# Low parts of split operands by accumulating DMAs on GpSimd, and a new list of priorities for the order, in a decoder trunk kernel

## The chip, the cores and the metric

The kernel runs on one core of one Trainium2 chip. The metric is device time in microseconds (us) from the launch of the program to its end, as a median over runs; lower is better. Beside it stands one execution under the hardware profiler, which gives the start and end of nearly every instruction on the five engines: TensorE (PE; its weight loads are shown as PEld), VectorE (DVE), ScalarE (ACT), GpSimd (POOL) and SyncE (SP, which here issues DMAs only).

## The reference

One layer of a decoder trunk on a sequence of 1024 tokens with 1024 channels, all in float32. The input is normalised, projected to 6 x 256 columns, given to four mixers of 256 channels each, projected back, added to a scaled copy of its own input and normalised; then comes a gated feed-forward net with a short causal convolution, and again a sum and a norm.

```
h  = x @ w_in + b_in              # 1024 x 1536: S5 | conformer value, gate | RG-LRU gate, input | query
A  = s5_mixer(...)                # complex diagonal state space, scan over time, GLU
B  = conformer_conv(v, g, ...)    # GLU, causal depthwise conv of 31 taps, group norm, swish, pointwise
C  = rglru_branch(xg, xr, ...)    # conv of 4 taps, block-diagonal gates, scan, gelu gate
M  = memory_cross_attention(q, mem, w_kv)   # 4 heads, 256 memory tokens
x  = layer_norm(alpha * x + concat(A, B, C, M) @ w_out, ...)
u  = causal_dwconv(x @ w_up);  ffn = (val * gelu(gt)) @ w_down        # d_ff = 2816, conv of 3 taps
x  = layer_norm(alpha * x + ffn, ...)
```

## The kernel before

**Stages.** Eight tiles of 128 tokens are loaded (`x0` to `x7`), normalised, turned by 64 PE transposes of 128x128 into a channel-major copy in PSUM, and split. Every large product takes float32 operands as a high part (rounded to the PE's fp32r type, `xh`, `wh`, `mxh`) and a low part (what the rounding left, `xl`, `wl`, `mxl`), and adds three passes: high x high, high x low, low x high (`mm3`). The in-projection runs over 12 column blocks of 128 (`in_mm`, n = 0 to 11; names `in_0`, `in_1` are the two halves of a block in PSUM), 48 matmuls of 128x512 each. Between its blocks stand the mixers: S5 (`s5_setup`, `s5_weights`, `s5_states`: PE products `vr`, `vi` of the turned input `ut`, scans `s5r`, `s5i` on VectorE, then `yp` products), the RG-LRU (`xr`, its four-tap convolution `xc`, gates `gt`, scan `gs`, output `lg`), the conformer (31 taps, of which 60 multiply-adds `acc` of 1.27 us run on VectorE and the rest on PE as `cc`; group norm with the products `cvar` and `cb` around a GpSimd power `crs`), and attention (`kps` and `vps` are keys and values of the memory, `sc`, `pt`, `ot` scores, transposes and outputs). Then the out-projection (`out_mm`, tiles `op`, i = 0 to 7 blocks of tokens, 8 k-steps), its residual `r1` and norm, and the feed-forward net as two Strassen-like products of seven block products each (`ux`, `ua`, `ub` up, `dna` to `dnc` down), whose operand sums run on VectorE.

**The low part.** In `split_w` a weight block of 128x1024 that a DMA has brought to `ws` is rounded to `wh` (by ScalarE or VectorE) and VectorE subtracts: `wl = ws - wh`. The same subtraction makes the low parts of the mixers' outputs: `put` (S5 glu and RG-LRU), `conf_out` and `attn_out`. In `residual` the input tile is reloaded, VectorE multiplies it by `g0r` and adds the row `bor` (names `r<-r,g0r` and `r<-r,bor`).

**What sets the order.** All work is first recorded in a `Plan`, as operations with a cost, their dependences and their buffers. `run` then places them one after the other, on each engine the operation that can start soonest and, within 0.1 us, the one with the largest critical path plus a number from the table `BOOST`, which has an entry for each part of the program (`in_mm`, `attn0`, `residual3`, ...). Operations recorded with `either` (all plain copies) go to ScalarE or to VectorE as the plan finds it. Each engine then issues its list strictly in that order, so an instruction that waits holds up all that stands behind it on its engine; SP's and GpSimd's lists of DMAs too. All instructions are emitted from one line, so every row of the profile says L405, and rows are told apart by their tiles.

Of the kernel before, what the change touches and what calls it, by code (L numbers as in the profile page):

```python
# [12 lines left out]
F32 = mybir.dt.float32  # L13
F32R = mybir.dt.float32r
I32 = mybir.dt.int32
AF = mybir.ActivationFunctionType
ALU = mybir.AluOpType
# [18 lines left out]
for _n, _w in (("b_in", 12), ("g0", 8), ("b0", 8), ("b_glu", 2), ("cv_w", 62), ("cv_b", 2),  # L36
# [18 lines left out]
TABLE = {AF.Exp: "exp", AF.Sigmoid: "sigmoid", AF.Gelu_apprx_tanh: "gelu", AF.Silu: "silu", AF.Sqrt: "sqrt", AF.Sin: "sin"}  # L55
TICK = 10240 / 3

BOOST = {"attn0": 109000, "attn1": -40000, "attn2": 27000, "attn3": -5000, "attn4": -35000, "attn5": 111000, "attn6":
# [18 lines left out]
         "up_post": 60000, "up_prep": 3500, "up_sums": 6500, "worse": 76}  # L77
LATENCY = {"tensor": 0, "vector": 120, "scalar": 150}


# [8 lines left out]
class Plan:  # L89
# [82 lines left out]
    def add(self, eng, method, a, kw, chain=None):  # L172
        aps = [v for v in list(a) + list(kw.values()) if hasattr(v, "ap") and hasattr(v, "offset")]
        out = kw.get("out", a[0] if a else None)
        outs = [out] + ([kw["accum_out"]] if "accum_out" in kw else [])
        ins = [v for v in aps if not any(v is o for o in outs)]
        o = self.open
        if o is None or o.eng not in (None, eng):
            o = Op()
            o.eng, o.calls, o.cost, o.lat, o.succ, o.npred, o.tiles, o.table, o.bytes, o.dge, o.part, o.work = eng, [], 0, 0, {}, 0, [], None, 0, 0, self.name, []  # L180
            o.alts = {}
            o.idx = len(self.ops)
            self.ops.append(o)
            if self.open is not None:
                self.open = o
        elif o.eng is None:
            o.eng = eng
        o.calls.append((eng, method, a, kw))
        if method == "dma_start":
            o.cost += 1000 if eng == "gpsimd" else 60  # L190
            o.dge += eng != "gpsimd"
            n = 4
            for v in out.shape:
                n *= v
            o.bytes += n
        else:
            kc = dict(kw, is_t=method == "transpose")
            o.cost += self.cost(eng, method, out, ins, kc, None)
            if eng == "tensor":
                o.work.append(self.work)  # L200
        if method == "activation":
            f = a[2] if len(a) > 2 else kw["func"]
            o.table = TABLE.get(f, o.table)
        for rw, aps in (("r", ins), ("w", outs)):
            for v in aps:
                self.touch(o, v, rw)
        if chain is not None:
            p = self.chains.get(chain)
            if p is not None and p is not o:
                self.edge(p, o)  # L210
            self.chains[chain] = o
        return o
# [67 lines left out]
    def run(self, order):  # L280
# [30 lines left out]
        while len(done) < n:  # L311
# [50 lines left out]
            if o.bytes:  # L362
                if o.dge:
                    dge = max(dge, st) + 453 * o.dge
                bus = max(bus, max(st, dge if o.dge else 0) + 650) + o.bytes / 360
                end = bus + 900
            for t in o.tiles:
                left[t] -= 1
                if left[t] == 0:
# [54 lines left out]
def trunk(ctx: ExitStack, tc: tile.TileContext, x, memT, w_kv, w_in, vecs, s5p, s5_d, w_glu, w_pw, w_ri,  # L424
# [96 lines left out]
    def times(out, src, by):  # L521
# [5 lines left out]
                    [("scalar", "activation", (out[:, a, :], src if flat else src[:, a, :], AF.Copy), dict(scale=by[:, a:a + 1]))  # L527
                     for a in range(n)])

    wst = {}  # L530

    def load_w(key, src):
# [1 line left out]
        sync.dma_start(t, src)  # L534
        wst[key] = t

    def split_w(key):

        s = wst.pop(key)
        hi, lo = unit(f"wh_{key}", dtype=F32R), unit(f"wl_{key}", dtype=F32R)  # L540
        copy(hi, s)
        dve.tensor_sub(lo, s, hi.bitcast(F32))
        return hi, lo

    def mm3(o, ah, al, bh, bl, first, last):
# [321 lines left out]
    @part('in_prep')  # L867
    def in_prep(n):
        if n < 12:
            load_w(("in", n), w_in[IN_ORDER[n]])  # L870
            wsp[n] = split_w(("in", n))

    hcv, acc = [], []

# [85 lines left out]
    def put(kt, src):  # L960
        for h in range(2):
            s = src[:, h * H:(h + 1) * H]
            copy(mxh[h][kt], s)
            dve.tensor_sub(mxl[h][kt], s, mxh[h][kt].bitcast(F32))

    @part('lru_out{}')
    def lru_out(ct):
# [139 lines left out]
    @part('attn_out{}')  # L1107
    def attn_out(h):
        dh, dl = mxh[h].pair(3), mxl[h].pair(3)
        copy(dh, oT[h])  # L1110
        dve.tensor_sub(dl, oT[h], dh.bitcast(F32))


    cn = []
# [30 lines left out]
    def conf_out():  # L1145
        for h in range(2):
            c = slice(h * H, (h + 1) * H)
            for ct in range(2):
# [4 lines left out]
                y = unit(f"ycv{ct}{h}", (P, H))  # L1153
                copy(y, ps, None, V("b_pw", ct))
                copy(mxh[h][2 + ct], y)
                dve.tensor_sub(mxl[h][2 + ct], y, mxh[h][2 + ct].bitcast(F32))


    wgp = unit("wgp", (P, 4, 256))
# [68 lines left out]
    @part('out_weights')  # L1228
    def out_weights(ks):
        for k in ks:  # L1230
            load_w(("out", k), w_out[k])
            wo[k] = split_w(("out", k))

    @part('out_mm{}')
    def out_mm(i, ks):
# [17 lines left out]
    def residual(i):  # L1253
        r = unit(f"r1_{i}")
        sync.dma_start(r, res0[i])
        dve.tensor_mul(r, r, g0r)
        dve.tensor_add(r, r, bo)
        res.append(r)
    for i in range(SPLIT):
        residual(i)  # L1260
# [494 lines left out]
```

## Time and profile before

| | |
|---|---|
| median of the runs | 1012.2 us (three runs, 1011.1 to 1012.95) |
| the profiled execution's own time | 1008.47 us |
| its span in the profile | 1006.7 us |
| PE busy | 960.8 us, 95% of the span |
| VectorE busy | 886.7 us, 88% |
| ScalarE busy | 454.8 us, 45% |
| GpSimd busy | 33.9 us, 3% |
| DMA | 113.10 MB, 32.0% of the 16 engines' span |
| mean granted clock of PE | 0.984 of full speed |

The span is the time from the first to the last instruction that the profiler saw; 1.8 us of the execution lie around it. A share of busy time is a mean over stages: PE is full over long stretches and idle in a few, and only these stretches can give time back without less work on PE. The granted clock says at what share of full speed PE was allowed to run.

### The profile page before, as it was taken

Reading aid. Unit: us, or ns where it says so; the run is one execution under the profiler, and the core shown is the slowest. Engines: PE = TensorE matmul, PEld = TensorE weight load, DVE = VectorE, ACT = ScalarE, POOL = GpSimd, SP = SyncE. Lnnn points to the kernel's source line nnn. Section 1 sums busy time; section 2 is a strip of 40 time slices with the busy share of each in tenths; the row PEclk is TensorE's granted clock in tenths of the full one; section 3 lists DMA queues with packets and bytes.
Section 4 is the critical chain, followed back from the end, with each engine's and each line's share of the span. In section 5 each row is a group of like instructions: output and inputs, shape, how many; then the busy total and the mean of one; then the engine's idle time right before and its main releaser. Section 6 shows DMA issues by size and latency. Waiting matters only on the chain. (4 is left out here: it accounts for less than half of the span.)

```text
span 1006.7 us, 12071 instructions
## 1 busy us (share of the span) xinstructions
PE 960.8 (95%) x4524; PEld 783.3 (78%) x4524; DVE 886.7 (88%) x1325; ACT 454.8 (45%) x659; POOL 33.9 (3%) x52
## 2 busy tenths in 40 slices
PE   5999985999999998999999999999999999999994
PEld 4878874776788876888888888888888888888883
DVE  8999998999877899998887887887877999997998
ACT  5444141899710255554554544554444532363410
POOL 2200000002000100000000000000000000000001
PEclk9999997999999999999999999999999999999997
DMA  9622021245112323132221221221115664123643
GB/s 359 269 63 84 21 58 41 84 151 168 59 42 93 121 80 118 71 139 71 84 105 63 84 105 63 85 104 63 63 42 210 229 211 132 66 73 126 213 153 126
DMA packets 43483, 113.10 MB, mean 112 GB/s; under 512 B 6256, under 2 KB 10368, under 8 KB 43424
## 3 DMA queue, kind: packets, MB, share of 16 engines
q1 hardware_dynamic: 43424, 112.33, 32.0%
q8 instruction: 35, 0.57, 0.2%
q14 instruction: 24, 0.20, 0.1%
HBM read 87.60 MB, written 24.12 MB: 111 GB/s over the span
## 5 line engine op out<-in xcount | busy, mean ns | idle before, releaser
L405 DVE SCALAR_TENSOR_TENSOR acc<-sg,vec,acc 128x1023 f32<-128x1023 f32 (+29 forms) x60 | 75.9, 1266 | 0.5
L405 DVE SCALAR_TENSOR_TENSOR up<-cv,vec,up 128x1023 f32<-128x1023 f32 (+1 forms) x44 | 56.2, 1278 | 2.8 <-ACT up L405 2.8
L405 PE MATMUL ux<-t4h,wd 128*128 128x512 f32 x176 | 57.8, 389 | 0.0
L405 ACT ACTIVATE up<-cv,vec 128x1024 f32<-128x1024 f32 x22 | 27.4, 1244 | 52.6 <-DVE cv L405 52.6
L405 DVE SCALAR_TENSOR_TENSOR up<-cg,vec,up 128x511 f32<-128x511 f32 (+1 forms) x44 | 33.0, 749 | 16.0 <-ACT up L405 15.4
L405 POOL TENSOR_TENSOR rs_n<-ve_n,mhalf 128x1 f32<-128x1 f32 x24 | 20.6, 886 | 769.9 <-DVE ve_n L405 765.0
L405 ACT ACT_TABLE_LOAD x27 | 34.6, 1283 | 16.2 <-PE in L405 12.2
L405 DVE TENSOR_TENSOR cg<-ux,u 128x512 f32<-128x512 f32 x22 | 15.2, 690 | 28.8 <-PE ux L405 28.8
L405 ACT ACTIVATE up<-cg,vec 128x512 f32<-128x512 f32 x22 | 17.9, 814 | 45.6 <-DVE cg L405 44.4
L405 PEld LDWEIGHTS ux<-t4h,wd 128*128 128x128 f32 x176 | 33.0, 188 | 6.9
L405 DVE TENSOR_TENSOR up<-up,up 128x1024 f32<-128x1024 f32 (+1 forms) x28 | 31.1, 1110 | 6.0 <-ACT up L405 5.9
L405 ACT ACTIVATE x1r<-tp 128x512 f32<-128x512 f32 x13 | 7.5, 606 | 60.4 <-PE tp L405 52.3
L405 PE MATMUL ux<-t4l,wd 128*128 128x512 f32 x88 | 34.2, 389 | 0.0
L405 DVE SCALAR_TENSOR_TENSOR up<-ux,vec,up 128x512 f32<-128x512 f32 x44 | 32.9, 747 | 0.1
L405 ACT ACTIVATE u<-ux 128x512 f32<-128x512 f32 x44 | 25.9, 588 | 11.7 <-PE ux L405 11.7
L405 PE MATMUL dna<-d1t,d1s 128*128 128x512 f32 x132 | 30.1, 389 | 0.0
L405 PE MATMUL dnb<-d2t,d2s 128*128 128x512 f32 x132 | 30.1, 389 | 0.0
L405 PE MATMUL dna<-d6t,d6s 128*128 128x512 f32 x132 | 30.1, 389 | 0.0
L405 PE MATMUL dnc<-d5t,d5s 128*128 128x512 f32 x132 | 30.1, 389 | 0.0
L405 PE MATMUL dna<-d7t,d7s 128*128 128x512 f32 x132 | 30.1, 389 | 0.0
L405 PE MATMUL dnc<-d3t,d3s 128*128 128x512 f32 x132 | 30.1, 389 | 0.0
L405 PE MATMUL dna<-d4t,d4s 128*128 128x512 f32 x132 | 30.1, 389 | 0.0
(1511 smaller groups left out, 2969.0 us busy)
## 6 DMA issues: line engine op xcount, KB each, us to landing
hd<-up SPq DMA_DIRECT2D x18, 512.0 KB, 3.1
hf<-hd SPq DMA_DIRECT2D x18, 512.0 KB, 4.6
r<-res SPq DMA_DIRECT2D x16, 512.0 KB, 4.5
x<-in SPq DMA_DIRECT2D x8, 512.0 KB, 7.0
res<-x SPq DMA_DIRECT2D x8, 512.0 KB, 9.3
res<-r SPq DMA_DIRECT2D x8, 512.0 KB, 2.8
out<-r SPq DMA_DIRECT2D x16, 256.0 KB, 2.1
d2w<-in SPq DMA_DIRECT2D x11, 256.0 KB, 3.2
```

What stands on the lines that cost most here:

```text
L405: getattr(getattr(self.nc, eng), method)(*(self.place(v) for v in a), **{k: self.place(v) for k, v in kw.items()})
```

## The change

**Low parts.** A new helper `low_part` writes `lo = -hi` (ScalarE or VectorE, as the plan chooses) and then has GpSimd issue a DMA from the float32 source onto `lo` that adds as it writes. It replaces the subtraction for 18 weight blocks of 512 KB (in-projection blocks 2 to 11, whose source is read again from HBM, and the eight out-projection blocks), for eight halves of 128x512 (RG-LRU and conformer outputs) and for the two attention outputs of 128x1024. In-projection blocks 0 and 1 and the S5 output keep the subtraction.

**Residual.** The addition of `bor` in `residual` becomes an accumulating DMA of 512 KB, eight in all. Together 36 DMAs are issued from GpSimd's queue, which had none.

**Planner.** An accumulating DMA is entered with twice its bytes and 2500 ns to landing after its bytes instead of 900; the table `BOOST` has other numbers throughout.

```diff
@@ in the planner
-            o.bytes += n
+            o.bytes += n * (1 + ("accum_op" in kw))
...
-                end = bus + 900
+                end = bus + (900 if o.dge else 2500)
@@ new helper, and split_w
+    def low_part(lo, hi, src):
+
+        h = hi.bitcast(F32)
+        plan.either([("scalar", "activation", (lo, h, AF.Copy), dict(scale=-1.0))], [("vector", "tensor_scalar_mul", (lo, h, -1.0), {})])
+        pool.dma_start(lo, src, accum_op=ALU.add)
...
-        dve.tensor_sub(lo, s, hi.bitcast(F32))
+        if src is None:
+            dve.tensor_sub(lo, s, hi.bitcast(F32))
+        else:
+            low_part(lo, hi, src)
@@ put, attn_out, conf_out
-            dve.tensor_sub(mxl[h][kt], s, mxh[h][kt].bitcast(F32))
+            low_part(mxl[h][kt], mxh[h][kt], s)
...
-        dve.tensor_sub(dl, oT[h], dh.bitcast(F32))
+        low_part(dl, dh, oT[h])
...
-                dve.tensor_sub(mxl[h][2 + ct], y, mxh[h][2 + ct].bitcast(F32))
+                low_part(mxl[h][2 + ct], mxh[h][2 + ct], y)
@@ residual
-        dve.tensor_add(r, r, bo)
+        pool.dma_start(r, bo, accum_op=ALU.add)
@@ the table, one of its lines before and after
-         32000, "residual0": 80000, "residual1": 204000, "residual2": 48000, "residual3": -14000, "residual4": -63000,
+         "out_mm3": 55000, "out_mm4": -42000, "out_mm5": -25500, "out_mm6": 70000, "out_weights": 87000, "residual0":
```

**How the order moves, on PE in the S5 stage.** Before, PE's list has, behind the scores `sc` of attention step 1, the RG-LRU gates `gt` and then the S5 output products `yp`; the next projection block (9) comes behind all of them:

```order
L405 MATMUL yp_225_1448<-ut_161_1336,m_154_548 128x128 x4
L405 MATMUL sc_228_1454<-kT_586,qT_188_1070 128x256
L405 MATMUL sc_229_1456<-kT_586,qT_188_1070 128x256
L405 MATMUL gt_215_1478<-xc_213_1302,wri_1413 128x512
L405 MATMUL gt_216_1482<-xc_213_1302,wri_1413 128x512
L405 MATMUL yp_222_1415<-s5sr_681,d_re_601 128x128
L405 MATMUL yp_223_1441<-s5sr_681,d_re_601 128x128
```

In the changed kernel the same two gate rows are followed at once by the 48 matmuls of block 9 (`in_0_242`, `in_1_243`), then the other gate rows, the scores, and half of block 10; only behind these stand the `yp` products of the scans:

```order
L405 MATMUL ot_206_1459<-pT_202_1450,vv_1385 64x128 x8
L405 MATMUL gt_215_1472<-xc_213_1298,wri_1442 128x512
L405 MATMUL gt_216_1475<-xc_213_1298,wri_1442 128x512
L405 MATMUL in_0_242_1481<-xh_0_42_311,wh_('in', 9)_208_908 128x512
...
L405 MATMUL in_1_243_1525<-xh_3_108_469,wl_('in', 9)_209_1059 128x512
L405 MATMUL gt_218_1561<-xc_213_1298,wri_1442 128x512
L405 MATMUL sc_228_1564<-kT_1328,qT_188_1040 128x256
...
L405 MATMUL yp_225_1577<-ut_161_1354,m_154_154 128x128 x4
L405 MATMUL in_0_266_1585<-xh_0_42_311,wh_('in', 10)_240_1158 128x512
```

So one and a half projection blocks (72 matmuls) now stand between the gates and the products that need the scans. The 32 steps of keys and values (`kps`, `vps`), which stood between blocks 0 and 1 and their transposes, moved the other way, to just ahead of the S5 products `vr`; and all 64 transposes now stand ahead of the first projection matmul.

**On VectorE in the same stage.** Before, the third and last tap of the RG-LRU convolution `xc_213`, on which the gates wait, stands behind the S5 scans and four of their products:

```order
L405 SCALAR_TENSOR_TENSOR s5i_1421<-ez,s5i_1421 128x128 x8
L405 TENSOR_TENSOR s5sr_681<-s5r_1346,mdc_882 128x8x127
L405 TENSOR_TENSOR s5t_1357<-s5i_1421,mds_860 128x8x127
L405 TENSOR_TENSOR s5si_683<-s5r_1346,mds_860 128x8x127
L405 TENSOR_TENSOR s5sr_681<-s5sr_681,s5t_1357 128x8x127
L405 SCALAR_TENSOR_TENSOR xc_213_1302<-xr_212_1253,vec,xc_213_1302 128x1021
L405 TENSOR_TENSOR s5t_1357<-s5i_1421,mdc_882 128x8x127
L405 TENSOR_TENSOR wl_('in', 10)_241_1480<-ws_('in', 10)_239_921,wh_('in', 10)_240_1298 128x1024
```

In the changed kernel it stands ahead of the first S5 product on VectorE:

```order
L405 SCALAR_TENSOR_TENSOR xc_213_1298<-xr_212_1191,vec,xc_213_1298 128x1021
L405 SCALAR_TENSOR_TENSOR acc_182_1105<-sg_181_943,vec,acc_182_1105 128x1005
L405 TENSOR_REDUCE atm_197_1344<-sc_195_1331 128x2
...
L405 TENSOR_SCALAR wl_('in', 11)_265_1391<-wh_('in', 11)_264_1383 128x1024
L405 TENSOR_TENSOR s5r_1399<-vr_165_1365,mdc_1100 128x512
```

The negation of block 11's high part (`TENSOR_SCALAR wl`) is one of the new instructions.

**On GpSimd, from the out-projection's weights to the norms behind it.** Its list had in this place only the two powers `crs` and the `rs_n` powers of the layer norm. Now:

```order
L405 DMA wl_('out', 1)_403_1859<-in 128x1024
L405 TENSOR_TENSOR crs_292_1900<-cve_291_1898,mhalf 128x16
L405 TENSOR_TENSOR crs_301_1923<-cve_300_1907,mhalf 128x16
L405 DMA mxl_1_326_2049<-ycv_324_2023 128x512
...
L405 DMA r_3_454_2411<-bor_2196 128x1024
L405 TENSOR_TENSOR rs_n_0_423_2508<-ve_n_0_422_2505,mhalf 128x1
L405 TENSOR_TENSOR rs_n_1_433_2547<-ve_n_1_432_2537,mhalf 128x1
L405 TENSOR_TENSOR rs_n_2_449_2589<-ve_n_2_448_2587,mhalf 128x1
L405 DMA r_7_515_2604<-bor_2196 128x1024
```

The powers of the norms stand behind the accumulating DMAs of the mixers' outputs and the residuals, and each waits until those ahead of it have been issued.

## Rows read from the trace of the kernel before

**Rows 1.** Windows of the span, busy time of each engine and granted clock

```profile
core 0: us, PE busy (x) PEld busy (x) DVE busy (x) ACT busy (x) POOL busy (x), PEclk, DMA share, GB/s
0.00:20.00 20.00, 8.76 (x38) 7.74 (x39) 15.30 (x41) 8.94 (x11) 5.54 (x13) 1.00 0.90 345
40.00:60.00 20.00, 18.53 (x87) 15.41 (x88) 20.00 (x61) 6.97 (x9) 4.26 (x16) 1.00 0.26 84
143.30:173.60 30.30, 16.29 (x133) 13.09 (x132) 26.74 (x47) 7.76 (x16) 0.00 (x0) 0.75 0.20 47
149.10:162.80 13.70, 11.73 (x96) 10.20 (x96) 10.27 (x23) 4.15 (x8) 0.00 (x0) 0.78 0.24 48
162.80:174.70 11.90, 3.68 (x5) 1.17 (x5) 11.90 (x17) 0.69 (x1) 0.00 (x0) 0.61 0.03 9
...
380.00:400.00 20.00, 17.34 (x68) 13.30 (x67) 19.79 (x30) 11.30 (x16) 0.00 (x0) 0.91 0.32 106
```

**Rows 2.** Waits of PE: what it waited for, total, times, longest

```profile
PE tp L405 <- ACT x L405: 9.5, 1, 9.5
PE gt L405 <- issue: 8.2, 1, 8.2
PE vr L405 <- DMA ut<-us: 3.9, 1, 3.9
PE ux L405 <- DVE wsb0l L405: 2.3, 1, 2.3
```

**Rows 3.** Timeline of VectorE, 165 to 176 us: start, length, operation

```profile
169.64 1.27 DVE L405 SCALAR_TENSOR_TENSOR xc<-xr,vec,xc 128x1021 f32<-128x1021 f32 x1
...
171.96 1.22 DVE L405 TENSOR_TENSOR wl_('in', 10)_241_1480<-ws_('in', 10)_239_921,wh_('in', 10)_240_1298 128x1024 fp32r<-128x1024 f32 x1
173.10 1.21 DVE L405 TENSOR_TENSOR s5si<-s5si,s5t 128x1016 f32<-128x1016 f32 x1
```

**Rows 4.** Timeline of PE at the gate matmuls, 171 and 203 us

```profile
171.02 3.75 PE L405 MATMUL gt<-xc,wri 128*128 128x512 f32 x4 [8.22 <-issue]
...
203.39 3.59 PE L405 MATMUL gt<-xc,wri 128*128 128x512 f32 x8
```

**Rows 5.** Timeline of PE around the first projection matmul

```profile
15.18 3.63 PE L405 MATMUL tp<-ident,x 128*128 128x128 f32 x16 [1.71 <-DVE x L405]
18.51 0.54 PE L405 MATMUL in<-xh,wh_('in', 0)_64_245 128*128 128x512 f32 x1
```

**Rows 6.** Tiles of the removed and added operations: duration ns min/median/max

```profile
L405 DVE TENSOR_TENSOR mxl<-lg,mxh x4: 683/684/691, 207.6 to 243.6; 128x512 fp32r<-128x512 f32 x4
...
L405 ACT ACTIVATE mxh<-oT x1: 1061/1061/1061, 234.5 to 234.5; 128x1024 fp32r<-128x1024 f32 x1
L405 DVE CAST mxh<-oT x1: 695/695/695, 310.0 to 310.0; 128x1024 fp32r<-128x1024 f32 x1
...
L405 DVE TENSOR_TENSOR r<-r,bor x8: 1207/1221/1227, 260.3 to 354.6; 128x1024 f32<-128x1024 f32 x8
```

**Rows 7.** Window from the start to the first tap copy

```profile
0.00:222.30 222.30, 195.07 (x1027) 157.73 (x1028) 212.21 (x370) 108.66 (x155) 14.41 (x34) 0.96 0.35 123
```

**Rows 8.** Timeline of PE, conformer taps and norm

```profile
221.07 3.59 PE L405 MATMUL cc<-acc,vec 128*128 128x512 f32 x8
...
231.89 1.09 PE L405 MATMUL cb<-ident,crb 128*128 128x128 f32 x8
```

**Rows 9.** Tile crs, the group-norm scale

```profile
L405 POOL TENSOR_TENSOR crs<-cve,mhalf x2: 2905/2906/2907, 226.6 to 229.5; 128x16 f32<-128x16 f32 x2
L405 DVE COPY crb<-crs x2: 683/686/689, 230.4 to 233.8; 128x1024 f32<-128x1024 f32 x2
```

**Rows 10.** DMA issues: KB each, median us from issue to landing

```profile
ws_('in', 4)_155_391<-in SPq DMA_DIRECT2D x1, 512.0 KB, 10.9
...
ws_('in', 11)_263_947<-in SPq DMA_DIRECT2D x1, 512.0 KB, 3.2
```

**Rows 11.** Timeline of PE, first matmul of the output projection

```profile
256.08 0.79 PE L405 MATMUL op<-wh_('out', 2)_381_1569,mxh 128*128 128x512 f32 x1
```

More of the change, by code (lines that the diff above doesn't have):

```diff
@@ L56 @@
 TICK = 10240 / 3
-BOOST = {"attn0": 109000, "attn1": -40000, "attn2": 27000, "attn3": -5000, "attn4": -35000, "attn5": 111000, "attn6":
[18 rows of a table removed]
-         "up_post": 60000, "up_prep": 3500, "up_sums": 6500, "worse": 76}
+BOOST = {"attn0": 139500, "attn1": 108000, "attn2": 44500, "attn3": -50500, "attn4": -41000, "attn5": 152000, "attn6":
[18 rows of a table added]
+         138000, "up_prep": 5500, "up_sums": 5500, "worse": 103}
 LATENCY = {"tensor": 0, "vector": 120, "scalar": 150}
@@ L535, in load_w, with split_w @@
         wst[key] = t
-    def split_w(key):
+    def split_w(key, src=None):
         s = wst.pop(key)
@@ L870, in in_prep @@
             load_w(("in", n), w_in[IN_ORDER[n]])
-            wsp[n] = split_w(("in", n))
+            wsp[n] = split_w(("in", n), w_in[IN_ORDER[n]])
     hcv, acc = [], []
@@ L1231, in out_weights @@
             load_w(("out", k), w_out[k])
-            wo[k] = split_w(("out", k))
+            wo[k] = split_w(("out", k), w_out[k])
     @part('out_mm{}')
```

34 rows, old and new, of the table BOOST are left out of this document.

## Prediction

> **What bounds the kernel now.** I read the windows of the span first: they say in which stages PE, busy for 95% of the span, is idle or slow. At full speed a window of 20 us shows 20.00 us of PE. From 60 to 140 us and from 400 to 980 us it does, so no edit can gain there. Time is lost in four places. At the start PE is busy for 8.76 us of 20, and 1.47 us are missing between 40 and 60 [rows 1]. From 143.3 to 173.6 us PE is busy for 16.29 of 30.30 us: 14.0 us idle, and the granted clock is 0.75 [rows 1]. From 380 to 400 us 2.7 us are missing. Behind the last matmul VectorE ends the final norm; no edit touches that, and the rows of that tail stand in nearly the same order in both kernels.
>
> The second view is the waits of PE. The large one inside the program is `gt` with 8.2 us, then `vr` with 3.9 us (the turned input of S5 comes back from DRAM) [rows 2]. The first has "issue" as its cause, so I looked in VectorE's timeline for what was late: the last tap of `xc` starts at 169.64 us and takes 1.27 us [rows 3], and the gate matmuls start at 171.02 us [rows 4]. VectorE, not PE, was the bound here: it is busy for 26.74 of these 30.30 us and for 212.21 of the first 222.30 us [rows 1, 7]. What is behind `gt` on PE's list, three blocks of projection among it, waited too.
>
> The clock cost as much again as half the idle time. Four gate matmul records took 3.75 us at 171 us, eight took 3.59 us at 203 us [rows 4]: PE ran at 1.2 instead of 2.4 GHz, behind the idle time. Between 149.1 and 174.7 us PE was busy for 11.73 + 3.68 = 15.4 us [rows 1]; half of that, 7.7 us, is what the lower clock cost.
>
> **The change part by part.**
>
> *VectorE's work ahead of the taps.* The point where the taps' matmuls `cc` need the finished `acc` is the next place where PE meets VectorE. Counted in the order, 17 weight subtractions and two half-size ones are gone ahead of it. A full one occupies VectorE for 1.14 us (171.96 to 173.10 [rows 3]) and a half about 0.6 (0.684 less the same overlap [rows 6]): 20.6 us. Added are 12 negations and four roundings of 128x1024 and one half negation on VectorE. The trace has no negation; the rounding of the same shape takes 0.695 us [rows 6], about 0.6 from start to start, while a plain two-operand pass would be 1.14. A negation reads one operand, so I take 0.6: 10.0 us. The difference is 10.6 us; if it costs 1.14, 4 us. Other steps (a product of `mdf`, of `pe`, `lq`, two of the scan, copies) moved behind the point, worth 8.6 us by the same row-to-row distances. VectorE's work to the point falls by 19.2 us, from 212.2 to 193.0. Its idle time was 10.1 us, 3.6 of it in the S5 stage, which the new order avoids; 6.5 stay, and I add 2.0 for the later start below: the taps are complete at about 201.5 us.
>
> *PE's way to the same point.* Before, `cc` starts at 221.07 us [rows 8]. Of the rows ahead of it the second set of gates (3.59 us), a score step (1.1) and four transposes (0.5) stand behind it after the change, so its equal in the old order is 215.9 us. The new order puts one and a half projection blocks (72 matmuls at 90 per 20 us, 16 us) between the gates and the `yp` products, which covers the scans, and the keys and values (32 steps, about 13 us) ahead of `vr`, which covers the way of `ut` through DRAM. With the 14.0 us of idle and 7.7 us of slow clock gone PE would be there at 194.2 us.
>
> *The start.* All 64 transposes now stand ahead of the first projection matmul, which started at 18.51 us behind 32 of them [rows 5]. Thirty-two more take 7.3 us at 16 in 3.63 us [rows 5], and the last tile's load and norm must come first; I put it at 29 us. By then 14.5 us of PE work is done, so 14.5 are idle, against 11.2 + 1.5 = 12.7 in the windows [rows 1]: a loss of 1.9. Bounds: 0 to 6 (a further tile late). The 3 MB of `mem` and `wkv`, which shared the first 40 us, come later; that is where this term could be smaller. PE is then at `cc` at 196.1 us and VectorE at 201.5: VectorE still decides, and PE waits 5.4 us, spread over `yp` and `cc`.
>
> *Group norm.* Its power `crs` takes 2.906 us, then VectorE copies for 0.686 [rows 9]. From the first `crs` at 226.6 us to the end of the copy are 4.5 us; `cb` came at 231.89 [rows 8] behind other matmuls. In the new list 3 to 4 us of matmuls stand there: a loss of 1.0. `crs` now also stands behind the weight DMAs on GpSimd, whose negations end some rows before it.
>
> *The DMAs' own price.* No accumulating DMA is in the trace. From below I take 3.2 us to landing, a load of the same 512 KB with the queues quiet, from above 10.9 us, the slowest load [rows 10]. Hidden or not is decided by the slack: a projection block lasts 10.9 us and each low part is asked for one block later or more; the first output matmul came at 256.08 us [rows 11], 12.4 earlier by the sum below, and the conformer's last negation stands on VectorE some 22 us of rows behind the taps, at about 223.5. Four transfers have 20 us there, 5 each in a row. I cost them at nothing, cover being those blocks; without it the price is below. GpSimd was busy for 14.41 of the first 222.30 us [rows 7], so its time is free.
>
> A row shows that VectorE copies, such as the roundings of 0.695 us [rows 6], stand thick in this stretch. The Trainium skill ("SBUF — State Buffer", section "Who interferes with whom") says of such copies that a DMA issued from GpSimd is stalled because its descriptors cannot be written meanwhile; by it each transfer would wait for the end of a copy, under 1 us by the row, and the sum would lose up to 1 us at the last transfer of a stage. No row here can show it, and the sum goes without.
>
> *Residual.* Eight additions of 1.22 us [rows 6] leave VectorE, 9.8 us. In the output stage VectorE had room, PE being the bound there, so I count 0. The `rs_n` powers now stand behind the residual DMAs; eight matmul groups cover them.
>
> *380 to 400 us.* The same splits on VectorE meet the same `ux` products; the order of them is new but their distance to PE is not larger, so I count 0 (bounds -3 to +3).
>
> *Sum.* -14.0 - 7.7 + 1.9 + 5.4 + 1.0 = -13.4, and 1.0 less for small waits on ScalarE where VectorE and PE now arrive together: -12.4 us. Against the profiled execution's 1008.47 us that is 996. The median of the runs shown is 3.7 us above it, and the time after is again a median: **1000 us**.
>
> **The rivals.** A measurement of this kernel tells a change of about 0.2% (2 us) from none.
>
> *The dip comes back elsewhere.* VectorE and PE meet with almost no slack at `yp`, `cc` and `cb`. If PE is idle for some us there it drops to the lower clock as it did at 145 us, and half of the busy time behind it is lost again. With 7.7 us of slow clock kept and 2 us more idle, the gain is 3: 1009 us. For it: the low clock followed 3.9 us of idle. Against it: where VectorE is the bound, slow matmuls ahead of it cost little.
>
> *Accumulating DMAs too slow: slower than before.* The place is the conformer's output: four transfers in a row on one queue, then `op`. They have 20 us. At 10.9 us each in series [rows 10], 43.6 us, PE waits 23.6, which is 11 us more than the gain: 1023 us. It decides from (20 + 12.4) / 4 = 8.1 us each. For it: nothing in the trace bounds the transfers but loads, and an addition reads its target too. Against: transfers of one queue overlap: in the first window the loads moved 345 GB/s [rows 1], 1.5 us for each 512 KB, though single ones needed many times that to land.
>
> *VectorE holds GpSimd up.* VectorE is busy for 212.21 of the first 222.30 us [rows 7]. If GpSimd issued only between its passes, and each of the 36 transfers stood 0.695 us, one rounding, on PE's path, the time would be 25 us above the forecast, 1025; from 0.34 us each the gain is gone. Against it: each low part is asked for a block later, so most of such a wait is covered. That GpSimd can be held up like this is the rule of the SBUF page of the Trainium skill named above.
>
> *Nothing moves.* PE is idle as much, only elsewhere: VectorE was the bound to 222 us, and if the negations cost 1.14 and the late start 6, VectorE comes to the taps at 211.5 us, still 4 us better, and a further dip takes that: 1012 us.
>
> *More is gained.* VectorE comes with less idle than 6.5 us, PE goes through, and the 2.7 us at 380 go too: 990 us.
>
> **How the numbers follow.** Forecast (994 to 1005): 0.46. More gained (below 994): 0.15. Dip elsewhere (1005 to 1010): 0.17. Nothing moves (1010 to 1014): 0.08. Slow transfers: 0.10. GpSimd held up: 0.04. The predicted time is that of the forecast; its own range is 994 to 1005. For 8 in 10 the range leaves out the lowest part of the gains and the far part of the slow case: 989 to 1013. Faster 0.78, same 0.08, slower 0.14.
>
> **What would show it right or wrong.** In the profile after: the windows from 140 to 180 us at 20.00 of PE and clock 1.00, and `gt` no longer among PE's waits; the first `in` matmul near 29 us; a wait of some us at `yp` or `cc` on VectorE; `cb` waiting for `crb`; no wait of PE on a GpSimd DMA; VectorE's total lower by 20 to 40 us (28 rows of 1.22 and eight of 0.684 are removed, 39.6 us; up to 18 of negations come back). The prediction is wrong if PE waits for DMAs onto `wl` or `mxl`, if the clock row shows a new stretch below 0.9, or if GpSimd's list delays `crs` or `rs_n`.

## Result and the profile after

The changed kernel takes 996.09 us in the median of four runs (995.25 to 997.22), the kernel before 1011.65 us beside it (1010.37 to 1012.95, four runs). The ratio is 0.9847, with a 95% interval of 0.983 to 0.9864: faster by 15.6 us, or 1.5%. The profiled execution took 995.25 us, with a mean granted clock of 0.991.

The head of the page after: the span, the busy time of the engines and the queue of the accumulating DMAs.

```profile
span 993.5 us, 12187 instructions
...
PE 958.7 (96%) x4524; PEld 783.4 (79%) x4524; DVE 863.3 (87%) x1316; ACT 454.0 (46%) x669; POOL 66.0 (7%) x88
...
q0 software_dynamic: 5184, 16.78, 9.2%
```

VectorE's work fell from 886.7 to 863.3 us and GpSimd's rose from 33.9 to 66.0. The new 16.78 MB are the 36 accumulating DMAs.

PE's waits after, the answer to [rows 2]; of those left out none is on a DMA from GpSimd.

```profile
PE tp L405 <- ACT x L405: 10.5, 1, 10.5
PE tp L405 <- DVE x L405: 4.8, 1, 4.8
PE vr L405 <- DMA ut<-us: 3.1, 1, 3.1
PE tp L405 <- DVE r L405: 2.0, 1, 2.0
...
PE cc L405 <- DVE acc L405: 0.3, 1, 0.3
```

The 8.2 us of `gt` and the 2.3 of `ux` are gone, and `vr` still waits for `ut`. The windows after, against [rows 1]:

```profile
0.00:20.00 20.00, 4.69 (x21) 4.09 (x22) 14.68 (x44) 7.47 (x8) 7.66 (x17) 1.00 0.92 348
20.00:40.00 20.00, 18.97 (x96) 15.60 (x95) 19.84 (x52) 19.19 (x29) 3.58 (x5) 1.00 0.91 320
...
140.00:160.00 20.00, 16.54 (x149) 13.88 (x148) 15.63 (x23) 7.57 (x17) 1.73 (x2) 1.00 0.67 161
...
200.00:220.00 20.00, 19.69 (x89) 12.90 (x88) 10.58 (x16) 9.67 (x15) 9.20 (x6) 0.83 1.07 265
...
380.00:400.00 20.00, 20.00 (x90) 16.57 (x89) 19.50 (x26) 12.80 (x15) 0.00 (x0) 1.00 0.29 105
```

The S5 stage, 14.0 us idle at clock 0.75 before, now loses 3.46 us between 140 and 160 at clock 1.00. The start is worse. A new slow stretch stands between 200 and 220, where PE is hardly idle and the clock is 0.83. PE's timeline shows the steps that the prediction had put numbers on:

```profile
28.35 0.50 PE L405 MATMUL in<-xh,wh_('in', 0)_64_241 128*128 128x512 f32 x1 [0.31 <-ACT x0f L405]
...
150.29 0.44 PE L405 MATMUL vr<-ut,w 128*64 128x128 f32 x4 [3.05 <-DMA ut<-us]
...
159.54 1.96 PE L405 MATMUL gt<-xc,wri 128*128 128x512 f32 x4 [0.41 <-DMA wri<-in]
...
203.19 1.88 PE L405 MATMUL cc<-acc,vec 128*128 128x512 f32 x4
205.36 1.96 PE L405 MATMUL cc<-acc,vec 128*128 128x512 f32 x4 [0.30 <-DVE acc L405]
207.23 4.45 PE L405 MATMUL cvar<-vec,csq 128*128 128x2 f32 x32
...
218.53 0.60 PE L405 MATMUL cb<-ident,crb 128*128 128x128 f32 x4
...
249.47 0.79 PE L405 MATMUL op<-wh_('out', 2)_381_1589,mxh 128*128 128x512 f32 x1
```

Four gate matmuls at 159.54 us take 1.96 us where they took 3.75 [rows 4]. The taps start 17.9 us earlier than in [rows 8], and their second half waits 0.30 us for VectorE. The first output matmul comes 6.6 us earlier than in [rows 11].

**The balance.** PE's idle time up to 400 us falls from 31.6 us (12.8 of it to 60 us, 14.0 from 140 to 180, 3.5 from 340 to 400) to 23.0 (16.3, 3.5 and 2.0): 8.5 us. From 400 to 960 us PE is busy for 560.00 of 560 us in both. The same 4524 matmuls take 960.8 us before and 958.7 after, 2.1 us less, most of which is the lower clock of before. The last 2.5 us lie at the end: behind the last matmul the kernel before needs 14.3 us (992.4 to 1006.7) and the changed one 11.8 (981.7 to 993.5). Together 13.1 of the 13.2 us by which the span fell.

### The profile page after: what moved, and what is told of

The parts are those of the page before. It is cut to its first block, busy times and chain, and to the rows that moved or that the text cites. A ratio compares the mean times of both kernels' runs of the same rounds, so it can differ in the third digit from the quotient of the medians.

```text
span 993.5 us, 12187 instructions
## 1 busy us (share of the span) xinstructions
PE 958.7 (96%) x4524; PEld 783.4 (79%) x4524; DVE 863.3 (87%) x1316; ACT 454.0 (46%) x669; POOL 66.0 (7%) x88
## 3 DMA queue, kind: packets, MB, share of 16 engines
q0 software_dynamic: 5184, 16.78, 9.2%
## 5 line engine op out<-in xcount | busy, mean ns | idle before, releaser
L405 POOL TENSOR_TENSOR rs_n<-ve_n,mhalf 128x1 f32<-128x1 f32 x24 | 18.1, 779 | 694.6 <-DVE ve_n L405 694.6
L405 DVE SCALAR_TENSOR_TENSOR up<-cg,vec,up 128x511 f32<-128x511 f32 (+1 forms) x44 | 33.0, 749 | 15.6 <-ACT up L405 15.0
L405 ACT ACTIVATE up<-cg,vec 128x512 f32<-128x512 f32 x22 | 17.9, 815 | 44.7 <-DVE cg L405 44.6
L405 PEld LDWEIGHTS dnb<-d2t,d2s 128*128 128x128 f32 x132 | 24.8, 188 | 5.1
```

Of the source, the lines that this page charges most:

```text
L405: getattr(getattr(self.nc, eng), method)(*(self.place(v) for v in a), **{k: self.place(v) for k, v in kw.items()})
```

## Experiments

The ratios are to the kernel before on the same chip, with their 95% intervals. All edits are made where the finished list of steps is issued, so each list keeps its order but for the rows that a diff names.

### Order alone, changes alone

The first kernel has the new order, and every low part and addition is VectorE's again (in it and in `w_sub` the low parts of the 18 weight blocks are formed as `hi - hi`, so they are left out of the result). In the diff `kinds` holds all three kinds of tile (`wl_` weights, `mxl` mixer outputs, `r1_` residual); the kernels that undo one kind have one in it.

```diff
...
+                if key in low and a[0].name.startswith(kinds):
+                    if a[0].name.startswith("r1_"):
+                        if "accum_op" in kw:
+                            eng, method, a, kw = "vector", "tensor_add", (a[0], a[0], a[1]), {}
+                    elif "accum_op" in kw:
+                        continue
+                    elif method in ("activation", "tensor_scalar_mul"):
+                        s = low[key] if a[0].name.startswith("mxl") else a[1]
+                        eng, method, a, kw = "vector", "tensor_sub", (a[0], s, a[1]), {}
                 getattr(getattr(self.nc, eng), method)(
```

> The changed kernel with its new order kept row for row, and the old operations put back in it: every low part is again a subtraction on VectorE, in the place of the negation, every residual sum again an addition on VectorE, and no DMA adds. (For the 18 weight blocks the subtraction takes the high part twice, so their low parts are zero; its shape and cost are those of before.) Theory A, order and edits need each other: ahead of the taps VectorE gets back 12 times about 0.5 us (negations that were its own) and 5 times 1.14 (negations that ScalarE did) and the two halves, some 12 us, and PE waits for it at the taps: 1005 to 1009 us. Theory B, the order alone makes the gain: 994 to 999. Theory C, the edits alone make it: 1010 to 1014.

Measured: 1008.55 us, 0.997 (0.9951 to 0.9988). The order alone is worth 3 us. (The execution in its profile took 1005.54 us.) PE's wait at the taps in this kernel, which was 0.3 us in the changed one:

```profile
PE cc L417 <- DVE acc L417: 5.2, 1, 5.2
```

Four windows, first of the kernel before, then of the order alone, then of the changed kernel (the first number after the length is PE's busy time):

```profile
0.00:60.00 60.00, 47.18 (x223) 39.90 (x224) 54.61 (x175) 31.86 (x40) 14.41 (x34) 1.00 0.73 281
140.00:180.00 40.00, 25.99 (x227) 19.27 (x227) 36.15 (x58) 14.81 (x25) 0.00 (x0) 0.79 0.23 61
200.00:260.00 60.00, 59.15 (x312) 39.73 (x311) 56.30 (x81) 54.34 (x103) 5.78 (x2) 1.00 0.47 155
260.00:340.00 80.00, 80.00 (x425) 66.15 (x424) 64.23 (x90) 18.79 (x34) 4.60 (x6) 1.00 0.17 62
```

```profile
0.00:60.00 60.00, 43.14 (x201) 35.28 (x202) 54.80 (x174) 35.01 (x51) 14.77 (x34) 1.00 0.67 255
140.00:180.00 40.00, 35.97 (x229) 28.76 (x228) 38.12 (x57) 18.84 (x30) 0.00 (x0) 0.96 0.23 59
200.00:260.00 60.00, 53.42 (x289) 33.71 (x288) 51.08 (x80) 38.32 (x80) 5.78 (x2) 0.94 0.33 114
260.00:340.00 80.00, 77.13 (x378) 63.44 (x377) 72.02 (x96) 18.47 (x28) 3.31 (x6) 1.00 0.24 86
```

```profile
0.00:60.00 60.00, 43.66 (x204) 36.23 (x204) 54.42 (x175) 36.09 (x52) 19.05 (x39) 1.00 0.90 299
140.00:180.00 40.00, 36.54 (x237) 28.91 (x236) 34.92 (x56) 22.54 (x33) 3.13 (x3) 1.00 0.38 94
200.00:260.00 60.00, 58.77 (x337) 38.11 (x336) 48.67 (x79) 48.30 (x95) 17.07 (x15) 0.94 0.83 210
260.00:340.00 80.00, 80.00 (x369) 66.54 (x368) 59.51 (x84) 12.76 (x19) 9.43 (x13) 1.00 0.56 152
```

The order by itself repairs the S5 stage (25.99 to 35.97 us of PE). But it loses 4.0 us at the start, 5.7 from 200 to 260, where PE catches VectorE up at the taps, and 2.9 in the output stage. What the DMAs do is to give the last two back.

The second kernel has the old order with the 36 DMAs:

```diff
...
+                if src is not None:
+                    self.nc.vector.tensor_scalar_mul(self.place(a[0]), self.place(a[2]), -1.0)
+                    self.nc.gpsimd.dma_start(self.place(a[0]), self.place(src), accum_op=ALU.add)
+                    continue
```

> The kernel before with its old order kept row for row, and all 36 edits put into it: each low part is a negation on VectorE in the place of the subtraction and an accumulating DMA on GpSimd, each residual sum an accumulating DMA. Theory A: ahead of the late tap of xc stand eight weight subtractions that become negations, 0.54 us less each, so the gates come 4 to 5 us earlier and the idle time and slow clock shrink by that: 1005 to 1008 us. Theory B: no change, 1010 to 1014. Theory C: 994 to 999. A rival of all: transfers are too slow where the old order leaves less room, and PE waits for them: 1014 or more.

Measured: 1027.55 us, 1.0161 (1.0143 to 1.0178). The edits without their order make the kernel slower by 16 us, which I had given as the rival. Waits of PE, then of VectorE, in this kernel:

```profile
PE gt L418 <- issue: 7.3, 1, 7.3
PE tp L418 <- DVE r L418: 5.2, 2, 4.8
PE vr L418 <- ACT pe L418: 4.1, 1, 4.1
PE yp L418 <- DMA m<-ks: 2.8, 1, 2.8
```

```profile
DVE r L418 <- DMA r<-bor: 14.6, 5, 4.6
...
DVE wl_('out', 6)_394_1810 L415 <- DMA mxl<-lg: 4.0, 1, 4.0
```

The gates' wait stayed. Up to 143.4 us VectorE is busy for 131.35 us instead of 137.22, yet the last tap of `xc` starts at 174.21 instead of 169.64 us: what VectorE was spared became idle time, since the next pass on its list waits for PE (`oT` for `ot` 3.8 us, 1.9 before). And with the old list a pass that needs a transfer stands right behind it. By the profile only half of the loss is waiting: of the 19.8 us by which the span grows, to 1026.5, 9.9 are idle time of PE, and 9.9 are busy time for the same 4524 matmuls (970.7 instead of 960.8 us), at a mean clock of 0.976 instead of 0.984. To see what of the 16 us the residual makes, its eight additions went back to VectorE:

```diff
-                    self.nc.gpsimd.dma_start(self.place(a[0]), self.place(a[2]), accum_op=ALU.add)
-                    continue
+                    pass
```

> The order of before with the low parts of weights and mixer outputs changed, and the eight residual additions left on VectorE. Theory A: what made the edits in the old order 16 us slower is the r<-bor transfers, for which VectorE waited 14.6 us in five waits, since in the old order its next pass stands right behind them: without them 1012 to 1017 us. Rival: it is lost at the start and at the gates (PE's gt wait of 7.3 us stayed and moved 4.6 us later) and at 385 us: 1023 to 1028 us.

Measured: 1019.37 us, 1.0089 (1.0056 to 1.0122), between the two. About half of the 16 us is the residual's transfers. Of the rest my rival named the wrong places: PE is busy to 60 us for 46.34 us (47.18 before) and from 140 to 180 for 26.15 (25.99), but from 260 to 340 for 76.98 (80.00). There it waits 2.0 us for `glus` and 1.0 us for a transfer from `oT` onto `mxl`. Of the 8.5 us by which its span grows, 3.4 are busy time (964.2 instead of 960.8 us).

### One kind of edit undone

> The changed kernel and its order, with only the 18 weight blocks back to a subtraction on VectorE (of the high part from itself, so their low parts are zero; same shape and cost). Theory A: as order_only within 2 us, 1004 to 1009, since these are what stands ahead of the taps on VectorE. If instead the mixers' or the residuals' edits carry the gain: 995 to 998.

Measured: 1006.63 us, 0.9956 (0.9938 to 0.9973). With the weights' subtractions back the wait at the taps is 4.5 us, and PE is busy for 15.51 us from 200 to 220. The busy time of its page, and the wait:

```profile
PE 965.6 (96%) x4524; PEld 789.5 (79%) x4524; DVE 875.9 (87%) x1322; ACT 448.1 (45%) x663; POOL 49.2 (5%) x70
```

```profile
PE cc L417 <- DVE acc L417: 4.5, 1, 4.5
```

The wait is the smaller part of the loss. Of the 11.2 us by which the span grows over that of the changed kernel, to 1004.7, 3.7 are idle time of PE up to 400 us and 6.9 are busy time (965.6 instead of 958.7 us for the same matmuls). Some 4 of these 6.9 are the lower clock at the taps: it is 0.50 from 210.4 to 227.4 us, with PE busy for 14.80 us, where the changed kernel has 6.70 us at 0.50. In `order_only`, with a wait of 5.2 us, it is the other way round: of 10.3 us, 9.3 are idle time and 0.5 busy time. So what the clock adds to such a wait is not the same in each of these kernels.

> The changed kernel and its order, with only the eight residual sums back on VectorE, 8 times 1.14 us. Theory A: PE is the bound in the output stage, so nothing: 995 to 998. Rival, VectorE is the bound there too: up to 9 us more, 1001 to 1006.

Measured: 998.69 us, 0.9883 (0.9859 to 0.9906), 2.6 us above the changed kernel by the medians, 3.6 by the ratios. PE's idle time up to 400 us grows by 2.9 us: by 1.7 from 260 to 340 us, in the output stage, and by 0.9 from 200 to 260, where `cvar` waits 1.2 us for ScalarE's `csq`.

> The changed kernel with only the mixers' low parts formed by a subtraction on VectorE again. Two half-size ones of them stand ahead of the taps' matmuls, some 0.3 us of VectorE's time net, and the conformer's and the attention's stand where PE had 20.00 us in its windows. Theory A (only work ahead of the taps counts): 995 to 998 us. Rival (their transfers cover something, or VectorE's passes meet PE at the conformer's or attention's output): 999 us or more.

Measured: 998.36 us, 0.9876 (0.985 to 0.9902), some 3 us above the changed kernel by the ratios. The intervals of these two touch that of the changed kernel, so their sizes are rough. PE meets VectorE in small waits, `cc` 1.0, `ot` 0.6 and `pt` 0.6 us, and ScalarE in one, `cvar` 0.9. The weights carry most of the gain: undone by themselves they cost 10.5 us, the other two kinds 2 to 4 each. All three undone together (`order_only`) cost 12.5, so the three don't simply add up.

### What is left: the way of `ut`, and the slow clock

SyncE's queue in the changed kernel, where `ut` is loaded:

```profile
132.07 0.33 SPq L405 DMA_DIRECT2D wkv<-in  x1
132.93 11.54 SPq L405 DMA_DIRECT2D m<-ks  x16
144.51 4.60 SPq L405 DMA_DIRECT2D ut<-us  x2
```

Sixteen small copies stand ahead of the first half of `ut`, though its source `us` had been written from 62.6 and 73.4 us on. (A row's length runs from the first issue to the end of the last, with what lies between.) The next kernel lets ScalarE issue eight of them. The one after it puts two other matmul groups between the two halves of `cvar`, to see whether those 32 matmuls lower the clock; the third does both.

```diff
+                if eng == "sync" and a[0].name.startswith("m1") and a[1].name.startswith("ks"):
+                    eng = "scalar"
```

```diff
...
+        for name in ("gt100", "pt11"):
+            n = [n for n, v in enumerate(done) if v[2] == "tensor" and v[0].calls[0][2][0].name.startswith(name)][0]
+            done.insert(at + 1, done.pop(n))
```

> The changed kernel, with eight of the sixteen small DMAs that bring S5's kernel blocks from ks to m issued by ScalarE instead of SyncE. In the profile after, PE waits 3.1 us at vr for the turned input ut, whose load stands on SyncE behind all sixteen (11.5 us). Theory: the load is issued some 5 us earlier, the wait goes, VectorE gets vr 3 us earlier and comes to the taps 3 us earlier: 993 to 994 us. Rival: PE then only waits longer at a later place, 996.

Measured: 991.46 us, 0.9807 (0.9785 to 0.983). PE's timeline and SyncE's queue in it:

```profile
147.75 0.44 PE L407 MATMUL vr<-ut,w 128*64 128x128 f32 x4
```

```profile
133.22 7.77 SPq L407 DMA_DIRECT2D m<-ks  x8
142.87 0.83 SPq L407 DMA_DIRECT2D ut<-us  x2
```

The 3.1 us of `vr` are gone, `ut` is issued 1.6 us earlier (some 5 were expected; the eight copies left on SyncE stand 0.97 us apart) and `vr` starts 2.5 us earlier. `gt` now waits 1.3 us for `wri`, and `op` 1.5 us for a transfer from `lg` onto `mxl`. The taps start at 201.52 us, 1.7 earlier. But the new waits take all of it back: PE's idle time up to 400 us is 23.07 us, and 23.05 in the changed kernel; the time behind its last matmul is the same in both, too. The 3.7 us by which the span fell, to 989.8, are all in PE's busy time:

```profile
PE 954.9 (96%) x4524; PEld 780.4 (79%) x4524; DVE 862.9 (87%) x1316; ACT 454.3 (46%) x669; POOL 65.9 (7%) x88
```

It is 954.9 instead of 958.7 us for the same 4524 matmuls, and the clock is higher in two places: 0.91 instead of 0.83 from 200 to 220 us, and 1.00 instead of 0.97 from 340 to 400. So in this execution the rival came true (PE waits later), and the gain came by the clock, which its expectation had not named. It beats both kernels, and is 4.6 us faster than the changed one by the medians, 4.0 by the ratios, whose intervals meet at 0.983; no version here is faster beyond its interval.

> The changed kernel, with four transposes and one gate matmul of PE's list put between the two groups of 16 narrow matmuls (cvar, 2 columns wide). In the profile after, the clock of PE fell to half behind these 32, with no idle time ahead. Theory: with wide work between them, as in the kernel before, the clock stays at full and the 3.3 us of the window go: 993 to 994 us. Rival: what lowers the clock is the whole stretch of small work (cvar, pt, ot), and it falls anyway: 996.

Measured: 996.44 us, 0.9853 (0.9836 to 0.9871): no change, and from 207 to 219 us the clock is 0.72 as before. The split is not the remedy.

> m_act and cvar_split together. If both theories hold and do not cover each other: 990 to 992 us. If one of them gives nothing: 993 to 994.

Measured: 991.44 us, 0.9806 (0.9785 to 0.9827), as `m_act` alone. Here the clock is 1.00 from 200 to 220 us, but PE is busy for 19.11 instead of 19.71 us (`m_act`), so waits take back some of what that gives. Of the 3.8 us by which its span is below that of the changed kernel, 2.9 are busy time and 0.9 idle time.

### Slower transfers

How much slack have the DMAs? A power of 128x16 on GpSimd ahead of each delays it, and all behind it on that engine.

```diff
+                if "accum_op" in kw:
+                    for _ in range(1):
+                        self.nc.gpsimd.tensor_tensor(out=self.spin, in0=self.half, in1=self.half, op=ALU.pow)
```

> The changed kernel, with one more power of 128x16 on GpSimd (2.9 us) ahead of each of the 36 accumulating DMAs, so that each low part and residual is complete some 3 us later, more where several follow each other. Theory: their landing is covered by PE's other work, 0 to 2 us: 996 to 998. Rival of the prediction, slow transfers decide: 8 us or more, 1004 and above.

Measured: 1005.75 us, 0.9946 (0.9927 to 0.9965), 9.7 us above the changed kernel. Yet PE waits for no transfer onto `wl` or `mxl`. Its largest new wait:

```profile
PE cb L408 <- DVE crb L408: 6.1, 1, 6.1
```

`crb` waits 9.7 us for `crs`, the group norm's power, which stands on GpSimd behind ten delayed DMAs. The next two runs split the 36 into the eight for output weights and the 28 others.

> The changed kernel with one power of 128x16 (some 3.7 us in the earlier run) on GpSimd ahead of each of the eight transfers for output weights only. Theory A: the earlier run with 36 such powers lost 9.7 us because the group norm's power crs stands behind these eight on GpSimd: 1001 to 1004 us here, with a wait of PE at cb for crb of some 5 us. Rival (the loss came from the other 28 transfers): 996 to 998 us.

Measured: 994.13 us, 0.984 (0.9807 to 0.9873): no loss. `crb` waits 4.1 us for `crs`, but only 0.7 of it reaches PE. My theory, that these eight made the 9.7 us, is wrong.

> The same power ahead of the other 28 transfers (input weights, mixer outputs, residual) and none ahead of the eight for output weights. Theory A: their low parts are asked for a block later or more, so 996 to 999 us, with no PE wait for a transfer onto wl or mxl; two mixer transfers still stand ahead of crs. Rival (landing or the residual's transfers are on the path, or the powers on GpSimd cost VectorE time by themselves): 1002 us or more.

Measured: 1000.72 us, 0.9899 (0.987 to 0.9928), some 5 us more, between the two expectations. VectorE waits 9.8 us for `rs_n` (3.7 in the changed kernel), the residual's powers, which stand on GpSimd behind delayed transfers, and 2.5 us for a reload `r<-res`, which SyncE issues some 6 us later than in the changed kernel. From 260 to 340 us PE is busy for 76.26 instead of 80.00 us: `tp` waits 2.1 us behind `rs_n`, and `ot` 2.0 behind that reload. So delays are felt in two places. Eight of them ahead of `crs` are covered, ten (with all the others) are not; and the output stage loses by itself, one half through GpSimd's list, the other through the late reload, whose own cause I did not follow. Idle time is 3.8 of the 7.6 us by which the span grows, to 1001.1; 3.9 are busy time (962.6 us), as in `w_sub`.

## Why the prediction was right, point by point

The forecast was 1000 us, faster; 996.09 was measured, in its range.

- **VectorE's time ahead of the taps: shown.** This was the theory behind the gain, and `w_sub` and `order_only` show it: with the subtractions back PE waits 4.5 and 5.2 us at `cc`, and without them 0.3. The 11.2 us by which `w_sub` is longer are for the most part the clock behind such a wait and elsewhere, though, and not the wait. The negation takes 0.66 to 0.69 us on VectorE, 0.6 from start to start, as taken from the rounding. Mis-sized was the meeting point: I put PE at 196.1 us and VectorE at 201.5. PE came at 203.19, VectorE had been busy for 191.3 us by then (193.0 predicted), and they met there and at 205.36. The term of +5.4 us measured 0.3 as a wait; in its place PE was late by itself, by 7.1 us: 3.4 us more of idle time in the S5 stage, 1.6 more at the start (both below), and busy for 183.4 us up to that point instead of the 181.0 that the sum implies (215.9 less 27.2 us of idle time up to the taps of before, less 7.7), which is mostly the mis-sized clock.
- **S5 stage, -14.0 us of idle: 10.6 came.** The step "the keys and values ahead of `vr`, which covers the way of `ut` through DRAM" failed: 3.05 us were left. I took the way to be the transfer, and it was the queue ahead of it: the source had long been written, and the load was issued at 144.51 us, behind sixteen copies. I had counted matmuls, not what SyncE issues. `m_act` removes the wait, though not PE's idle time as a whole.
- **The slow clock, -7.7: mis-sized; 2.1 came in net.** I had taken all busy time from 149 to 175 us as run at the lower level, though the rows say 0.78 and 0.61 [rows 1]. The clock is at 0.50 only from 148.4 to 155.2 us and from 165.4 to 175.7, with PE busy for 5.58 and 4.68 us; half of that, 5.1 us, was lost. Nor is a full window one at full speed, as I had written: from 211 to 215 us after, PE is busy throughout at 0.50. A new slow stretch takes most of it back: at 0.50 from 210.5 to 217.2 us PE is busy for 6.70 us, which costs some 3.4. That makes 1.7 of the 2.1 us by which PE's busy time fell. So the rival of a dip elsewhere came true in part, and not behind idle time as I had it. (A short one at 384 us before, and one at 354 us after, cost some 1.6 us each.)
- **The start, +1.9: 3.5.** The first projection matmul came at 28.35 us (29 predicted), but PE had done 12.0 us of work by then, not 14.5. (The prediction's own numbers, 14.5 less 12.7, make 1.8, not 1.9.)
- **Group norm, +1.0:** `cb` shows no wait above 0.3 us. **380 to 400, 0:** the 2.7 us there went, and 2.0 came at 340 to 360 instead: 1.5 us gained from 340 to 400.
- **The tail, 0:** 2.5 us were gained. "The rows of that tail stand in nearly the same order" was not enough of a look: VectorE is busy throughout from 960 us to its end in both, and what it still has to do when PE ends sets the time. The order alone has 12.3 us there (991.5 to 1003.8), so this comes mostly from the order.
- **Residual, 0:** undone it costs some 2.6 us, 3.6 by the ratios. The output stage is not free of VectorE: 1.7 us of idle time come there, with PE's `tp` waiting 3.0 us in all for VectorE (2.0 in the changed kernel).
- **DMAs hidden, 0: right for this order.** At the rival's place, the conformer's output, the four transfers (`mxl<-ycv`, 256 KB each) landed 3.3 to 8.3 us after their issue. They were issued from 232.43 to 240.25 us, some 9 us later than I had put it, and overlapped: the last landed at 248.57, 0.9 us ahead of the first `op`. So the 20 us that I had given them were not there, and the rival failed because the transfers did not run one after the other; elsewhere landing took up to 17.6 us, beyond my upper bound of 10.9. The cover is thin: a transfer from `lg` landed at 259.56 us, and the matmul that waits 1.5 us for it in `m_act` began at 259.60. That the cover is this order's and not the edits' own is what `edits_only` shows.
- **VectorE holding GpSimd up.** The issue of such a DMA occupies GpSimd for 0.86 to 1.40 us beside VectorE's roundings of 0.69. The Trainium skill ("SBUF — State Buffer", section "Who interferes with whom") would have a part of that be a stall. The trace can't part the two, but eight delays of 2.9 to 4.6 us in `delay_out` cost nothing, so at these eight a stall of half a microsecond costs none either. For the other 28, whose larger delays did cost time, no run shows it.
- **The sum.** On the span, -10.6 of idle in the S5 stage, -2.1 of slow clock, +3.5 at the start, -1.5 from 340 to 400 us and -2.5 in the tail make -13.2, against -12.4 predicted: the size was nearly right, since the tail and the missing wait at the taps made up for the clock, the start and `ut`. That these misses cancelled is luck; the mechanism, VectorE's work ahead of the taps and the order around it, is not. The 996 forecast for the profiled execution was 995.25. The other 4 us of the miss are my last step: I added the 3.7 us by which the median of before stood above its profiled execution, and after it stands only 0.8 above.
- **The signs.** PE waits for no DMA onto `wl` or `mxl`, `gt` has 0.4 us left, and VectorE's total fell by 23.4 us, as written. But the window from 140 to 160 us has 16.54 us of PE, not 20.00, no wait of some us came at `yp` or `cc`, and one of the signs of a wrong prediction did come: a new stretch with the clock below 0.9 (0.83 from 200 to 220 us).

Open is the cause of the clock at 207 to 219 us. PE's idle time does not explain it, and the run of `cvar` by itself does not, since `cvar_split` did not change it. The rival named there, the whole stretch of small work (`cvar`, `pt`, `ot`), is left untested. In the two kernels with `ut` early, with the same work, the stretch is shorter or gone.

## What to carry to other kernels

Work that leaves a busy engine for a queue pays only if the order of the rest is made anew for it: here the order alone was worth 0.3%, the edits alone cost 1.6%, and the two together gained 1.5%. Before costing a transfer at nothing, count what stands ahead of it on the queue that issues it, and what stands behind it on the engine that issues it: the 3.1 us at `vr` and most of PE's idle time in the delayed kernels lay there, and not in PE's waits for low parts. And count the clock with the waits: in `w_sub` and `m_act` more of the change came by the clock than by idle time.

## What the runs showed of the hardware

An accumulating DMA from GpSimd is slow to land under load. Times from issue to landing: the median of the residual's eight (4.6 to 12.4 us one by one), and the fastest and two of the slowest of the weight blocks:

```profile
r<-bor POOLq DMA_DIRECT2D x8, 512.0 KB, 7.6
...
wl_('in', 9)_209_1059<-in POOLq DMA_DIRECT2D x1, 512.0 KB, 5.2
...
wl_('out', 7)_397_1800<-in POOLq DMA_DIRECT2D x1, 512.0 KB, 14.3
wl_('out', 0)_400_1815<-in POOLq DMA_DIRECT2D x1, 512.0 KB, 16.8
```

Those of 14 us and more are issued between 199 and 207 us, where the DMA share is 1.07. The Trainium skill ("DMA: Bandwidth & Descriptors", section "Anatomy of one DMA — SWDGE (gpsimd) path") gives about 2.0 us and the bytes at 436 GB/s, an estimate of 3.2 us for 512 KB. The fastest accumulating transfer of that size took 4.6 us here, and the measurement decides.

On SyncE's queue the 16 `m<-ks` copies of 8 to 64 KB take 11.54 us, 0.72 from one to the next (0.60 us each in the median); the issue of a load of 512 KB of `wkv` takes 0.33.

PE's clock fell with hardly any idle time ahead of it. Windows of the changed kernel:

```profile
207.00:209.00 2.00, 1.99 (x16) 1.67 (x15) 0.88 (x2) 2.00 (x5) 0.85 (x1) 1.00 1.14 281
...
211.00:213.00 2.00, 2.00 (x9) 1.76 (x9) 0.50 (x2) 0.00 (x0) 2.00 (x2) 0.50 1.11 287
213.00:215.00 2.00, 2.00 (x10) 0.73 (x9) 0.96 (x2) 0.62 (x1) 2.00 (x1) 0.50 1.06 246
```

From 160 to 207 us PE had waited 0.3 us, at 205 us; it is at the level of 2.4 GHz to 209 and at 1.2 GHz (0.50) from 211, busy throughout. A gate matmul takes up to 1179 ns there and 590 elsewhere.
